# First up-projection of a fused encoder layer: convolution and gate in tiles of 1024 columns, two-column copies on ScalarE

## The chip, the cores and the metric

The kernel runs on one core of one Trainium2 chip. The metric is device time in microseconds (us) of one execution, from the first to the last instruction of the core. The time before is 2424.99 us, the median of 3 runs (2424.58 to 2426.9). Engines are called by their names in the profile: PE is the matmul array (TensorE), PEld its weight load, DVE is VectorE, ACT is ScalarE, POOL is GpSimd, SP issues most DMAs.

## What is computed

The reference is one layer over 2048 positions of width 1024: a projection, two groups of heads side by side (A: spatial gating; B: attention with forgetting over 8 heads of width 64), an out-projection with a residual, and a feed-forward part whose up-projection is followed by a causal convolution over three positions and a gate. Cut to what matters here:

```python
s = jnp.einsum('bhtd,bshd->bhts', qi, k) * scale + ci[..., :, None] - c[:, :, None, :]
p = jax.nn.softmax(jnp.where(kpos[None, :] <= qpos[:, None], s, -jnp.inf), axis=-1)
out_b = jnp.einsum('bhts,bshd->bthd', p, v)
x = x + jnp.concatenate([out_a, out_b], axis=-1) @ w_out

def conv_ffn(h, w_up, w_conv, b_conv, w_down):       # D_FF = 2816
    a = h @ w_up                                     # (positions, 2 * D_FF)
    a = causal_depthwise_conv3(a, w_conv) + b_conv   # position t uses t, t-1, t-2
    g, val = jnp.split(a, 2, axis=-1)
    return (jax.nn.silu(g) * val) @ w_down
x = x + conv_ffn(rms_norm(x, norm_ffn_g), w_up, w_conv, b_conv, w_down)
```

## The kernel before, in words

**Arithmetic.** All data are 32-bit floats. A product is made of three matmuls on a high and a low part of each operand (high by high, high by low, low by high): `mm3` (L206 to L214) issues 24 matmuls of 128x512, all on L212, and calls `tick()` after each.

**Stages, by the trace of before.** Projections of both halves of the positions (0 to 584 us); `c_half`, the out-projection of the first 1024 positions with its norm and its transposes (584 to 726); `d_half`, the first up-projection, for the same 1024 positions (726 to 1419); `c_late`, the out-projection of the last 1024 positions (1419 to 1575); then the rest of the up-projection and the down-projection (to 2424).

**The attention as fill.** Attention of the B heads has no stage of its own. It is a generator, and `tick()` advances it by one step (`step()`) after every so many matmuls: four numbers in `RATES`, one each for the two halves of the projections, for `c_half` and for `d_half`. For each block of 512 queries and each head there are two parts:

- `b_max` (L759 to L797), the score sweep. One matmul (L774) for 128 queries against 512 keys, and one VectorE instruction that takes the row's minimum (L777, or L779 with the mask of the diagonal block). 16 of these for the last query block.
- `b_mix` (L799 to L866), over chunks of 128 keys, 16 for the last query block. Per chunk two matmuls for the scores (L821, L822), the exponential on ScalarE (L827), a split of it into two parts (ScalarE L832, VectorE L833), a running sum on VectorE (L835), and two matmuls with the values (L809, L810). At the end of a head the sums go through a small matmul (L851) and a reciprocal (L852); after the second head of a pair four transposes (L186, of the tile `rw` from ScalarE L857) and the store to `mixh` and `mixl` in DRAM follow.

`need(tb)` (L137) drives the generator until query block tb is through; it stands in `c_half`, in the last pair of `d_half` and in `c_late`. After the one in `c_late` the last query block is read back (`load_mix(3)`), and a matmul of `c_late` on tile `thi` needs that. Of the 384 matmuls of `c_late`, 228 don't need the attention of that block and stand in front of this point.

A scheduler makes each engine's final order from all of this at build time; steps of the attention carry a priority 100 places ahead. The order is then fixed: every engine takes its instructions one after the other.

**The first up-projection.** There are 22 pairs of channel groups (f for the gate, 22 + f for the value), and two blocks of 512 positions. `d_up` (L920 to L949) handles one pair and one block. For each of the two channel groups: `mm3` into a bank of PSUM; ScalarE copies it to a tile `a` of 514 columns (L931) and makes `t`, the same values times the third tap plus the bias (L932); VectorE copies the two columns of the block before from `halo` to the front of `a` (L933) and the last two columns of `a` to `halo` (L934), and adds the two other taps (L935, L936). Then the gate: tanh on ScalarE (L943), and two VectorE instructions (L944, L947), the second into the tile `va`, which a DMA issued on POOL stores after block 1 (L949). `d_half` (L951 to L976) calls `d_up` for f = 0 and 1 over block 0 and then over block 1, the same for f = 20 and 21, and for the 18 others block 0 and block 1 at once. After the first pair it closes the pools of `c_half` and opens a pool that gives the attention more buffers. `d_sums` prepares weights on POOL for a later stage.

The late up-projection, after 1575 us, already does its convolution and gate in tiles of 1024 columns; its lines L1225, L1282, L1283 and L1287 to L1289 are used below as a measure.

Of the kernel before, what the change touches and what calls it, by code (L numbers as in the profile page):

```python
# [8 lines left out]
F32 = mybir.dt.float32  # L9
# [23 lines left out]
RATES = [3.5, 4.0, 4.4, 3.6]  # L33
# [48 lines left out]
class Block:  # L82
    def __init__(self, ctx, tc, ins, out):
        self.ctx, self.tc, self.nc, self.a, self.out = ctx, tc, tc.nc, ins, out
        self.uid = 0
        self.count = 0
        self.late = []
        self.va = {}
# [831 lines left out]
    def d_up(self, f, wg, wv, b):  # L920
        nc, dp, pp = self.nc, self.dp, self.dpp
        outs = []
        hT = self.hT[b]
        for ch, (wh, wl) in ((f, wg), (NF + f, wv)):
            ps = self.til(pp, [P, TB], F32, "mm")
            self.mm3(ps, [wh[:, k, :] for k in range(KC)], [wl[:, k, :] for k in range(KC)],
                     [hT[0][:, k, :] for k in range(KC)], [hT[1][:, k, :] for k in range(KC)])
            t = self.til(dp, [P, TB], F32, "t")
            a = self.til(dp, [P, TB + 2], F32, "a")
            cc = slice(ch, ch + 1)  # L930
            nc.scalar.activation(a[:, 2:TB + 2], ps, AF.Copy)  # L931
            nc.scalar.activation(t, ps, AF.Identity, scale=self.cw2[:, cc], bias=self.cb[:, cc])  # L932
            nc.vector.tensor_copy(a[:, 0:2], self.halo[:, ch, :])  # L933
            nc.vector.tensor_copy(self.halo[:, ch, :], a[:, TB:TB + 2])  # L934
            nc.vector.scalar_tensor_tensor(t, a[:, 1:TB + 1], self.cw1[:, cc], t, op0=ALU.mult, op1=ALU.add)  # L935
            nc.vector.scalar_tensor_tensor(t, a[:, 0:TB], self.cw0[:, cc], t, op0=ALU.mult, op1=ALU.add)  # L936
            outs.append(t)
            if ch == f:
                spare = a
        g, v = outs  # L940

        th = spare[:, 0:TB]
        nc.scalar.activation(th, g, AF.Tanh, scale=0.5)  # L943
        nc.vector.scalar_tensor_tensor(g, th, 1.0, g, op0=ALU.add, op1=ALU.mult)  # L944
        if b == 0:
            self.va[f] = self.til(dp, [P, D], F32, "va")
        nc.vector.tensor_tensor(self.va[f][:, b * TB:(b + 1) * TB], g, v, op=ALU.mult)  # L947
        if b:
            nc.gpsimd.dma_start(self.act_d[0][f], self.va.pop(f))  # L949

    def d_half(self):  # L951

        units = lambda f: [self.load_unit(self.a["w_up"][c], P) for c in (f, NF + f)]
        for f0 in range(0, NF, 2):
            if 0 < f0 < NF - 2:
                for f in (f0, f0 + 1):
                    w = units(f)
                    self.d_up(f, *w, 0)
                    if f > f0:
                        self.d_sums(f // 2)  # L960
                    self.d_up(f, *w, 1)
                continue
            ws = [units(f0), units(f0 + 1)]
            for k in range(2):
                self.d_up(f0 + k, *ws[k], 0)
# [4 lines left out]
            for k in range(2):  # L970
                self.d_up(f0 + k, *ws[k], 1)
            if not f0:
                self.flush()
                self.accs.close()
                self.bx = self.bxs.enter_context(self.tc.tile_pool(name="bxpool", bufs=1, side="right", reuse_waits="tile"))
                self.more = True  # L976
    def d_sums(self, i):
# [506 lines left out]
    def run(self):  # L1484
# [15 lines left out]
        dstack = ExitStack()  # L1500
# [58 lines left out]
```

## Time and profile before

| | |
|---|---|
| time, median of 3 runs | 2424.99 us |
| time of the profiled execution | 2425.66 us |
| its span | 2424.0 us |
| PE busy | 2375.0 us, 98% |
| DVE busy | 1900.7 us, 78% |
| ACT busy | 1150.2 us, 47% |
| POOL busy | 335.8 us, 14% |
| mean granted PE clock | 0.991 |

The span is the time from the first to the last instruction that the profiler recorded; 1.66 us of the execution lie around it. "Busy" counts the time in which an instruction runs on an engine. Matmuls overlap each other on PE: one of 128x512 is shown with 0.39 us, but the next may start 0.23 us after it, so a PE that is 98% busy need not be at its peak. The granted clock tells at which share of its full rate the array was let run. A stretch of the span is shown by a row of ten or so numbers, each engine's busy time with its count of instructions. "Idle before <- X" is the time for which an engine stood still ahead of an instruction, and X is what let it go on.

### The profile page before, as it was taken

The numbers are of one execution on the slowest core, as the hardware profiler recorded it, in microseconds if no ns is written. First come the engines' busy times: TensorE is split into PE (matmuls) and PEld (weight loads), VectorE is DVE, ScalarE is ACT, GpSimd is POOL, SyncE is SP. The second block draws the span as 40 slices with busy tenths as digits, with TensorE's granted clock in tenths as the row PEclk, the third lists the DMA queues.
The fourth block names the chain that finished last, engine by engine and source line by source line (L and its number), as shares of the span: only waits on it lengthen the run. The fifth ranks groups of instructions, "written<-read, shape, count | busy, mean of one in ns | idle before, by whom it ended". The sixth has DMA issues, their size and how long they took to land.

```text
span 2424.0 us, 32411 instructions
## 1 busy us (share of the span) xinstructions
PE 2375.0 (98%) x11224; PEld 1974.9 (81%) x11224; DVE 1900.7 (78%) x3324; ACT 1150.2 (47%) x1986; POOL 335.8 (14%) x315
## 2 busy tenths in 40 slices
PE   9999999999999999999999999899999999999998
PEld 7888888988778888888887887688888887888887
DVE  5357777866679988999999887598888877957875
ACT  4235655432424444454454435465555455454444
POOL 4114130101123222222222010100000000000001
PEclk9999999999999999999999999899999999999999
DMA  8663536658545444444444453312222228538633
GB/s 263 185 242 99 176 95 175 173 170 294 174 156 195 163 143 152 144 155 148 150 159 151 164 200 132 122 53 88 86 79 87 87 91 308 163 100 299 202 119 123
DMA packets 234517, 379.56 MB, mean 157 GB/s; under 512 B 49944, under 2 KB 109464, under 8 KB 232928
## 3 DMA queue, kind: packets, MB, share of 16 engines
q1 hardware_dynamic: 229312, 353.36, 45.3%
q0 software_dynamic: 5040, 24.12, 2.5%
q8 instruction: 89, 1.46, 0.3%
q14 instruction: 76, 0.62, 0.1%
HBM read 283.82 MB, written 93.72 MB: 156 GB/s over the span
## 4 chain that ended last, share of the span: by engine, by line
PE 83%; DVE 6%; DMA 5%; issue 3%; ACT 1%; POOL 1%; SPq 0%; POOLq 0%; DVEq 0%; ACTq 0%
PE mm L212 39%; PE D L1373 14%; PE A L1171 3%; PE A L1172 3%; PE A L1173 3%; PE o L810 2%; PE o L809 2%; PE s L774 2%; PE s L822 2%; PE s L821 2%; PE B L1172 2%; PE B L1173 2%; PE B L1171 2%; DVE sum L835 1%; PE C L1171 1%
## 5 line engine op out<-in xcount | busy, mean ns | idle before, releaser
L212 PE MATMUL mm<-tlo,whi 128*128 128x512 f32 x896 | 352.4, 394 | 0.0
L212 PE MATMUL mm<-thi,whi 128*128 128x512 f32 x896 | 351.9, 393 | 0.5 <-DVE vn L520 0.5
L212 PE MATMUL mm<-thi,wlo 128*128 128x512 f32 x896 | 352.0, 393 | 0.0
L212 PE MATMUL mm<-whi,thi 128*128 128x512 f32 (+2 forms) x768 | 279.3, 364 | 16.3 <-DMA thi<-mixh 9.0
L212 PE MATMUL mm<-wlo,thi 128*128 128x512 f32 (+2 forms) x768 | 277.3, 362 | 2.0 <-DVE wlo L165 2.0
L212 PE MATMUL mm<-whi,tlo 128*128 128x512 f32 (+2 forms) x768 | 275.8, 360 | 0.4 <-DMA tlo<-mixl 0.4
L151 POOL TENSOR_SCALAR whi<-raw 128x1024 fp32r<-128x1024 f32 (+3 forms) x114 | 144.3, 1267 | 915.0 <-PE mm L212 743.0
L212 PEld LDWEIGHTS mm<-thi,whi 128*128 128x128 f32 x896 | 168.6, 188 | 34.5 <-issue 0.7
L212 PEld LDWEIGHTS mm<-tlo,whi 128*128 128x128 f32 x896 | 168.6, 188 | 33.6
L212 PEld LDWEIGHTS mm<-thi,wlo 128*128 128x128 f32 x896 | 168.6, 188 | 33.1
L212 PEld LDWEIGHTS mm<-whi,thi 128*128 128x128 f32 x768 | 146.9, 191 | 37.6 <-DMA thi<-mixh 10.0
L835 DVE TENSOR_TENSOR sum<-sum,e 128x512 f32<-128x512 f32 (+3 forms) x249 | 161.7, 650 | 13.6 <-ACT e L827 10.6
L212 PEld LDWEIGHTS mm<-wlo,thi 128*128 128x128 f32 x768 | 147.2, 192 | 22.5 <-DVE wlo L165 2.9
L212 PEld LDWEIGHTS mm<-whi,tlo 128*128 128x128 f32 x768 | 146.7, 191 | 21.8 <-DMA tlo<-mixl 1.3
L165 DVE TENSOR_TENSOR wlo<-raw,whi 128x1024 fp32r<-128x1024 f32 (+2 forms) x106 | 131.5, 1241 | 33.7 <-POOL whi L151 33.4
L827 ACT ACTIVATE e<-s 128x512 f32<-128x512 f32 (+3 forms) x207 | 105.2, 518 | 108.5 <-DVE s L825 46.9
L1373 PE MATMUL D<-wl,xh 128*128 128x512 f32 x368 | 141.5, 389 | 0.0
L1373 PE MATMUL D<-wh,xh 128*128 128x512 f32 x368 | 140.8, 389 | 0.2 <-DVE xo L1474 0.2
L833 DVE TENSOR_TENSOR pl<-e,ph 128x512 fp32r<-128x512 f32 (+3 forms) x195 | 123.5, 637 | 21.1 <-PE o L810 13.9
L1373 PE MATMUL D<-wh,xl 128*128 128x512 f32 x368 | 137.7, 389 | 0.0
L832 ACT ACTIVATE ph<-e 128x512 fp32r<-128x512 f32 (+3 forms) x195 | 105.4, 549 | 46.1 <-PE o L809 39.1
L931 ACT ACTIVATE a<-mm 128x512 f32<-128x512 f32 x88 | 52.6, 598 | 122.3 <-PE mm L212 118.3
(1837 smaller groups left out, 5756.4 us busy)
## 6 DMA issues: line engine op xcount, KB each, us to landing
raw<-in_w_up_dram SPq DMA_DIRECT2D x72, 512.0 KB
m<-kx SPq DMA_DIRECT2D x160, 136.0 KB
x<-act SPq DMA_DIRECT2D x84, 256.0 KB
m<-kx SPq DMA_DIRECT2D x67, 256.0 KB
v<-vd SPq DMA_DIRECT2D x67, 256.0 KB
raw<-in_w_in_dram SPq DMA_DIRECT2D x28, 512.0 KB
raw<-in_w_out_dram SPq DMA_DIRECT2D x24, 512.0 KB
tw<-in_w_down_dram SPq DMA_DIRECT2D x11, 1024.0 KB
```

The costliest lines, as they stand in the source:

```text
L151: self.cast_ins = self.nc.gpsimd.tensor_scalar(out, in_, 1.0, 0.0, ALU.mult, ALU.add).ins
L165: nc.vector.tensor_tensor(lo, raw, f32(hi), op=ALU.subtract)
L212: self.last_mm = self.nc.tensor.matmul(ps, lhsT=a[k], rhs=b[k], start=i == 0, stop=i == 3 * n - 1).ins
L827: nc.scalar.activation(e[:, c], ps[:, c], AF.Exp, scale=-1.0)
L832: nc.scalar.activation(ph[:, c], e[:, c], AF.Copy)
L833: nc.vector.tensor_tensor(pl[:, c], e[:, c], f32(ph[:, c]), op=ALU.subtract)
L835: nc.vector.tensor_tensor(total[:, c], total[:, c], e[:, c], op=ALU.add)
L931: nc.scalar.activation(a[:, 2:TB + 2], ps, AF.Copy)
L1171: mm(ps, lhsT=xh[:, ks], rhs=yh[:, k, :], start=fresh and k == 0, stop=False, **kw)
L1172: mm(ps, lhsT=xh[:, ks], rhs=yl[:, k, :], start=False, stop=False, **kw)
L1173: mm(ps, lhsT=xl[:, ks], rhs=yh[:, k, :], start=False, stop=k == 3, **kw)
L1373: nc.tensor.matmul(bank[t], lhsT=x[i][:, ts], rhs=w[k], start=fresh and j == 0 and i + k == 0, stop=last and i == 1, **kw)
```

## The change

1. **Wide tiles.** For f = 2 to 19 (`d_wide`) the two blocks of a channel pair now share one tile `a` of 1026 columns and one tile `t` of 1024. ScalarE still empties each bank of PSUM as before, 512 columns at a time, but the taps, the tanh and the two gate instructions are done once, over 1024 columns, after block 1. The result is written over the value's `t`, and the DMA stores it from there; the tile `va` is gone.
2. **The first and the last pair** (f = 0, 1, 20, 21; `d_blocks`) keep their order and their width of 512. Their four calls share two tiles `a` and the halves of one tile `t`.
3. **Two-column copies** (to and from `halo`) move from VectorE to ScalarE.
4. **Buffers.** Instead of 2 `a`, 4 `t` of 512 and 2 `va`, 2 `a` and 3 `t` of 1024, and one more of each in a pool that is opened after the first pair.
5. **Rates** of the attention fill: 3.8 instead of 4.0 matmuls for one step in the second half of the projections, 4.0 instead of 4.4 in `c_half`, 3.5 instead of 3.6 in `d_half`.

The program has 3042 VectorE instructions instead of 3326 and 2010 ScalarE instructions instead of 1924. PE, POOL and SP keep their numbers.

```diff
-RATES = [3.5, 4.0, 4.4, 3.6]
+RATES = [3.5, 3.8, 4.0, 3.5]
...
-    "ar": 4, "a": 2, "t": 4, ... "tw": 1, "s0": 1, "va": 2, "e+": 1, ...
+    "ar": 4, "a": 2, "t": 3, "a+": 1, "t+": 1, ... "tw": 1, "s0": 1, "e+": 1, ...
...
-    def d_up(self, f, wg, wv, b):
...
+    def d_channel(self, ch, w, b, a, t):
+        nc = self.nc
+        hT, (wh, wl) = self.hT[b], w
+        ps = self.til(self.dpp, [P, TB], F32, "mm")
+        self.mm3(ps, [wh[:, k, :] for k in range(KC)], [wl[:, k, :] for k in range(KC)],
+                 [hT[0][:, k, :] for k in range(KC)], [hT[1][:, k, :] for k in range(KC)])
+        nc.scalar.activation(a, ps, AF.Copy)
+        nc.scalar.activation(t, ps, AF.Identity, scale=self.cw2[:, ch:ch + 1], bias=self.cb[:, ch:ch + 1])
+
+    def d_conv(self, ch, a, t, n):
+        nc = self.nc
+        cc = slice(ch, ch + 1)
+        nc.scalar.activation(a[:, 0:2], self.halo[:, ch, :], AF.Copy)
+        nc.scalar.activation(self.halo[:, ch, :], a[:, n:n + 2], AF.Copy)
+        nc.vector.scalar_tensor_tensor(t, a[:, 1:n + 1], self.cw1[:, cc], t, op0=ALU.mult, op1=ALU.add)
+        nc.vector.scalar_tensor_tensor(t, a[:, 0:n], self.cw0[:, cc], t, op0=ALU.mult, op1=ALU.add)
+
+    def d_gate(self, th, g, v, out):
+        nc = self.nc
         nc.scalar.activation(th, g, AF.Tanh, scale=0.5)
         nc.vector.scalar_tensor_tensor(g, th, 1.0, g, op0=ALU.add, op1=ALU.mult)
+        nc.vector.tensor_tensor(out, g, v, op=ALU.mult)
+
+    def d_blocks(self, f, ws, b, a, t, out):
+        halves = t[:, 0:TB], t[:, TB:HALF]
+        for j in range(2):
+            self.d_channel(f + j * NF, ws[j], b, a[j][:, 2:TB + 2], halves[j])
+            self.d_conv(f + j * NF, a[j], halves[j], TB)
+        self.d_gate(a[0][:, 0:TB], *halves, out[:, b * TB:(b + 1) * TB])
+
+    def d_wide(self, f, ws, b):
         if b == 0:
+            self.wide = []
+        for j in range(2):
+            if b == 0:
+                self.wide.append((self.d_tile("a"), self.d_tile("t")))
+            a, t = self.wide[j]
+            self.d_channel(f + j * NF, ws[j], b, a[:, 2 + b * TB:2 + (b + 1) * TB], t[:, b * TB:(b + 1) * TB])
+            if b:
+                self.d_conv(f + j * NF, a, t, HALF)
         if b:
+            (a, g), (_, v) = self.wide
+            self.d_gate(a[:, 0:HALF], g, v, v)
+            self.nc.gpsimd.dma_start(self.act_d[0][f], v)
```

The scheduler lays out the whole program anew, so that the attention stands elsewhere among the matmuls. Two places show it. A number behind a tile's name only tells one tile of that name from another, and the lines of the changed kernel are one less than before for code that is the same (L211 for L212, L773 for L774, L776 for L777, L821 and L820 for L822 and L821).

**The tail of the attention, on PE.** The first place is the last matmul of `c_late` that can run before the last query block is read back, and what follows it. Before, the rows behind it are chunks of `b_mix`:

```order
L212 MATMUL mm_15131<-whi_14875,thi_14851 128x512
L212 MATMUL mm_15131<-wlo_14876,thi_14851 128x512
L212 MATMUL mm_15131<-whi_14875,tlo_14853 128x512
L810 MATMUL o_12972<-pl+_3050_13172,v+_3034_13116 128x512
L809 MATMUL o_12972<-ph+_3055_13193,v_13183 128x512
L821 MATMUL dn_13334<-t_49_401,m_48_400 128x512
L822 MATMUL dn_13334<-t_3076_13291,m_3079_13296 128x512
L821 MATMUL dn_13348<-t_49_401,m_48_400 128x512
```

In the changed kernel a score sweep comes first:

```order
L211 MATMUL mm_14821<-whi_14565,thi_14541 128x512
L211 MATMUL mm_14821<-wlo_14566,thi_14541 128x512
L211 MATMUL mm_14821<-whi_14565,tlo_14543 128x512
L773 MATMUL dn_12558<-m_47_399,t_49_401 128x512
L185 MATMUL s_12493<-ident,rw_12487 128x128 x4
L773 MATMUL s_12511<-m_48_400,t_49_401 128x512
L773 MATMUL s_12537<-m_48_400,t_49_401 128x512
L773 MATMUL dn_12564<-m_47_399,t_49_401 128x512
```

From there to the transposes of the last `rw`, which are followed by the matmuls that need the last query block, the order before has 16 matmuls of L821, 16 of L822, 20 of L809, 21 of L810 and 8 of L851: the end of one head and one whole head. In the changed kernel there are 14 of the score sweep (L773), the transposes of an earlier pair, 32 each of the four lines of `b_mix`, and 8 of L850: nearly a whole score sweep and two whole heads. The last 156 matmuls of the out-projection stand behind it in both.

**The convolution, on VectorE.** The second place lies in the middle of `d_half`. Before, the instructions of one channel and block stand between attention instructions of the same width, and the two-column copies stand among them:

```order
L933 COPY a_9792<-halo 128x2
L794 TENSOR_TENSOR t_50_402<-s_7945,rowsel 8x512
L934 COPY halo<-a_9719 128x2
L935 SCALAR_TENSOR_TENSOR t_9718<-a_9719,cols,t_9718 128x512
L835 TENSOR_TENSOR sum_7891<-sum_7891,e_7951 128x512
L936 SCALAR_TENSOR_TENSOR t_9718<-a_9719,cols,t_9718 128x512
```

In the changed kernel (L941 and L942 are the taps, L948 is the gate, L776 the minimum of the score sweep):

```order
L941 SCALAR_TENSOR_TENSOR t_10728<-a_10727,cols,t_10728 128x1024
L776 TENSOR_REDUCE part_8490<-s_8505 128x1
L942 SCALAR_TENSOR_TENSOR t_10728<-a_10727,cols,t_10728 128x1024
L776 TENSOR_REDUCE part_8490<-s_8511 128x1
L776 TENSOR_REDUCE part_8490<-s_8519 128x1
L847 TENSOR_TENSOR op_8476<-o_8243,op_8476 64x512
L948 SCALAR_TENSOR_TENSOR t_10728<-a_10727,t_10728 128x1024
```

The copies are gone from VectorE, and an attention instruction now waits for one tap of 1024 columns instead of 512; each tap stands once for two blocks.

More of the change, by code (lines that the diff above doesn't have):

```diff
@@ L87, in __init__ @@
         self.late = []
-        self.va = {}
         self.fill = None
@@ new lines, in d_tile @@
+    def d_tile(self, tag):
+        n = self.nd[tag] = self.nd.get(tag, -1) + 1
+        late = self.more and n % (BUFS[tag] + BUFS[tag + "+"]) >= BUFS[tag]
+        return self.til(self.d2 if late else self.dp, [P, HALF + 2 if tag == "a" else HALF], F32, tag + "+" if late else tag)
+    def d_channel(self, ch, w, b, a, t):
[6 more added lines that the diff above has]
+        nc.scalar.activation(t, ps, AF.Identity, scale=self.cw2[:, ch:ch + 1], bias=self.cb[:, ch:ch + 1])
@@ L957, in d_half @@
                     w = units(f)
-                    self.d_up(f, *w, 0)
+                    self.d_wide(f, w, 0)
                     if f > f0:
                         self.d_sums(f // 2)
-                    self.d_up(f, *w, 1)
+                    self.d_wide(f, w, 1)
                 continue
             ws = [units(f0), units(f0 + 1)]
+            out = [self.d_tile("t") for _ in range(2)]
+            t, a = self.d_tile("t"), [self.d_tile("a") for _ in range(2)]
             for k in range(2):
-                self.d_up(f0 + k, *ws[k], 0)
+                self.d_blocks(f0 + k, ws[k], 0, a, t, out[k])
             self.d_sums(f0 // 2)
```

32 lines of the change are left out of this document (6 added, 26 removed), and 2 rows, old and new, of the table BUFS.

## Prediction

> **What bounds the kernel now.** I read the page first, for the span and the busy time of the engines.
>
> ```profile
> span 2424.0 us, 32411 instructions
> PE 2375.0 (98%) x11224; PEld 1974.9 (81%) x11224; DVE 1900.7 (78%) x3324; ACT 1150.2 (47%) x1986; POOL 335.8 (14%) x315
> ```
>
> PE is busy nearly throughout, VectorE for 78%. As that is a mean over stages, the table by windows comes next: the out-projection of the first half, the up-projection that is changed, and the end of the attention. A row has start, end and length, the busy time of PE, PEld, DVE, ACT and POOL with counts, the granted PE clock, and the DMA's share and GB/s.
>
> ```profile
> 584.00:726.00 142.00, 132.93 (x599) 106.86 (x599) 93.62 (x172) 45.08 (x86) 30.20 (x31) 0.94 0.59 190
> 726.00:1419.00 693.00, 688.71 (x3166) 569.21 (x3165) 637.42 (x1194) 329.38 (x600) 153.58 (x125) 1.00 0.49 161
> 1492.00:1535.00 43.00, 31.74 (x126) 21.56 (x125) 26.02 (x50) 27.98 (x48) 3.49 (x8) 0.80 0.33 117
> 1496.20:1516.20 20.00, 17.58 (x63) 10.37 (x61) 18.93 (x37) 16.23 (x31) 0.00 (x0) 0.91 0.16 51
> 633.40:640.20 6.80, 5.28 (x13) 4.15 (x14) 0.00 (x0) 1.72 (x3) 0.10 (x1) 0.50 0.61 200
> ```
>
> In the up-projection VectorE is very full (637.42 of 693 us, 92%), yet PE stands idle for only 693 - 688.71 = 4.29 us, at the full clock. At the end of the attention it is the other way round: in 20 us from 1496.2, VectorE works for 18.93 us and PE has gaps, at a clock of 0.91. So the third view is the table of waits of PE, first for the up-projection alone (total, times, longest):
>
> ```profile
> PE o L810 <- DVE pl L833: 2.4, 3, 1.2
> PE s L851 <- DVE sum L835: 1.2, 1, 1.2
> PE s L821 <- DVE t L794: 0.6, 1, 0.6
> ```
>
> That is 4.2 us: nearly all the idle time of that stage is a wait for VectorE, and there is hardly any. For the whole span:
>
> ```profile
> PE mm L212 <- DMA thi<-mixh: 9.0, 2, 7.2
> PE o L810 <- DVE pl L833: 4.0, 6, 1.2
> PE s L822 <- DMA v<-vd: 3.2, 1, 3.2
> PE s L774 <- DVE part L777: 2.9, 4, 1.0
> ```
>
> The 7.2 us are the read of the last query block behind the attention's end. The timeline of PE shows that end (start, length, engine, line, tiles, and idle time with its releaser):
>
> ```profile
> 1491.74 0.39 PE L810 MATMUL o<-pl+_3050_13172,v+_3034_13116 128*128 128x512 f32 x1
> ...
> 1492.19 0.39 PE L821 MATMUL dn<-t,m 128*128 128x512 f32 x1
> 1492.42 0.39 PE L822 MATMUL dn<-t,m 128*128 128x512 f32 x1
> ...
> 1517.79 1.12 PE L186 MATMUL dn<-ident,rw 128*128 128x128 f32 x4 [1.22 <-ACT rw L857]
> ```
>
> Back to back, full matmuls start 0.23 us apart. From 1491.74, where the last matmul that needs no attention has just been issued, to 1517.79 there are 26.05 us of attention alone, which I call the tail. Its pace on VectorE:
>
> ```profile
> 1496.25 1.29 DVE L833 TENSOR_TENSOR pl<-e,ph 128x512 fp32r<-128x512 f32 x2 [0.37 <-ACT ph L832]
> ...
> 1500.24 0.68 DVE L835 TENSOR_TENSOR sum<-sum,e 128x512 f32<-128x512 f32 x1
> 1500.84 0.69 DVE L833 TENSOR_TENSOR pl+_3104_13377<-e,ph+_3103_13376 128x512 fp32r<-128x512 f32 x1
> ...
> 1515.85 0.29 DVE L835 TENSOR_TENSOR sum<-sum,e+_3162_13591 128x128 f32<-128x128 f32 x1
> 1516.17 0.69 DVE L848 TENSOR_TENSOR op<-o,op 64x512 f32<-64x512 f32 x1
> ```
>
> VectorE instructions start 0.60 us apart (1500.24 to 1500.84), and the 16 chunks of one head take it from 1496.25 to 1515.85 + 0.29 = 1516.14: 19.9 us, in which PE has only 64 matmuls of 0.23 us or less, at most 14.7 us. So the up-projection is bound by PE, the tail by VectorE.
>
> **VectorE and ScalarE, part by part.** The groups by line (count | busy in us, mean ns | idle before). First what is there now, then the same work at 1024 columns from the late up-projection, then ScalarE's tanh at both widths and its nearest tiny copy.
>
> ```profile
> L933 DVE COPY a<-halo 128x2 f32<-128x2 f32 x88 | 29.3, 333 | 0.4
> L934 DVE COPY halo<-a 128x2 f32<-128x2 f32 x88 | 20.0, 227 | 18.1 <-ACT a L931 17.8
> L935 DVE SCALAR_TENSOR_TENSOR t<-a,cols,t 128x512 f32<-128x512 f32 x88 | 69.8, 793 | 5.3 <-ACT t L932 5.3
> L936 DVE SCALAR_TENSOR_TENSOR t<-a,cols,t 128x512 f32<-128x512 f32 x88 | 70.8, 804 | 0.9
> L944 DVE SCALAR_TENSOR_TENSOR t<-a,t 128x512 f32<-128x512 f32 x44 | 32.8, 745 | 7.1 <-ACT a L943 6.9
> L947 DVE TENSOR_TENSOR va<-t,t 128x512 f32<-128x512 f32 x44 | 34.7, 789 | 0.3
> L1282 DVE SCALAR_TENSOR_TENSOR ts<-cv,cols,ts 128x1024 f32<-128x1024 f32 x44 | 55.8, 1283 | 29.8 <-ACT ts L1281 29.8
> L1283 DVE SCALAR_TENSOR_TENSOR ts<-cv,cols,ts 128x1024 f32<-128x1024 f32 x44 | 56.0, 1282 | 0.8
> L1288 DVE SCALAR_TENSOR_TENSOR ts<-cv,ts 128x1024 f32<-128x1024 f32 x22 | 26.8, 1219 | 0.0
> L1289 DVE TENSOR_TENSOR ts<-ts 128x1024 f32<-128x1024 f32 x22 | 26.8, 1218 | 0.0
> L943 ACT ACTIVATE a<-t 128x512 f32<-128x512 f32 x44 | 27.8, 632 | 87.0 <-DVE t L936 82.4 <-DVE rr L852 2.4 <-DVE mx L784 2.3
> L1287 ACT ACTIVATE cv<-ts 128x1024 f32<-128x1024 f32 x22 | 23.3, 1059 | 18.0 <-DVE ts L1283 18.0
> L1225 ACT ACTIVATE cv<-halo 128x4 f32<-128x4 f32 x22 | 4.5, 203 | 9.0 <-DVE ts L1288 8.2 <-DVE t2l L1013 0.6
> ```
>
> VectorE loses the six groups: 29.3 + 20.0 + 69.8 + 70.8 + 32.8 + 34.7 = 257.4 us. It gets 18 wide pairs of 2 x (1.283 + 1.282) + 1.219 + 1.218 = 7.57 us, 136.2 together, and 8 narrow ones (4 pairs, 2 blocks) of 2 x (0.793 + 0.804) + 0.745 + 0.789 = 4.73 us, 37.8 together. Net: 174.0 - 257.4 = -83 us, so about 554 of 693 us. ScalarE gets 2 x (18 x 2 + 4 x 2 x 2) = 104 copies of 0.203 us, 21.1 us, and its tanh falls from 27.8 to 18 x 1.059 + 8 x 0.632 = 24.1; net +17, on 329.38 of 693 us.
>
> On the path these 83 us are worth next to nothing: PE issues the same matmuls, and all that VectorE can give back there is the 4.2 us of waits. I take half, **-2 us**. Bounds: -4.3, the whole idle time of the stage, and +4, as many new waits. New ones are possible. On VectorE an attention instruction can now be queued behind a tap of 1.28 us (was 0.79), and PE's next matmul of that chunk waits for it. On ScalarE the copies follow their eviction on the same engine and wait for nothing else, but a tanh that waits for VectorE's taps (82.4 us of idle time now, in front of L943) waits for taps of 1.28 us, with the exponentials L827 queued behind it, for which L835, L833 and then PE's L809 wait. The cover is the 139 us in which VectorE will be free.
>
> The narrow pairs share tiles over their calls, so an eviction waits until the gate of the call before has read its tile. A call's two groups of 24 matmuls last 24 x 0.23 = 5.5 us each, its gate 0.632 + 0.745 + 0.789 = 2.2 us, so it is covered. If VectorE is late by 0.5 us in each of the 8 calls, that is again the +4. The store from `v`, with `t` free only when it is done, has a pair's 4 x 5.5 = 22 us of matmuls as its cover.
>
> **The out-projection of the first half** keeps its order nearly unchanged: **0 us**, with bounds of -6.6 (the 3.2 us wait for `v` goes, and with it half of the 6.8 us at clock 0.50, first fence) and +4 (as much again of the 3.2, rounded up).
>
> **The tail.** Here the order weighs. The changed kernel has a score sweep and two heads where before had about one. Two minima of a sweep, on the timeline of VectorE:
>
> ```profile
> 666.61 1.28 DVE L777 TENSOR_REDUCE part<-s 128x1 f32<-128x512 f32 x2
> ```
>
> The masked one by its group:
>
> ```profile
> L779 DVE CUSTOM_DVE_ANT_0 s<-s,mask 128x384 f32<-128x384 f32 (+3 forms) x113 | 53.3, 495 | 15.5 <-PE s L774 15.2
> ```
>
> Two minima take 1.28 us, one every 0.60. For 14 of a sweep: 10 x 0.60 + 4 x 0.5 = 8.0 us, and three instructions that close the pair of heads before (row 1516.17) at 0.60 = 1.8; together 10 us. Then two heads of 19.9. Ahead of all this I put 1 us, and at the end 1517.79 - 1516.14 = 1.65 us, as before. New tail: 1 + 10 + 39.8 + 1.65 = 52.4 us, against 26.05: +26.4.
>
> What was moved into the tail is gone from among the matmuls in front of it, where PE is the bound. Of the score sweep that is 14 matmuls, 10 full and 4 masked ones worth 2.5: 12.5 x 0.23 = 2.9 us. A head has 12 full chunks and 4 on the diagonal worth 2.5, so 14.5 x 4 = 58 full matmuls. Two heads make 116; before, one head and some 6 of the head ahead of it stood there, 64. The 52 more are 12.0 us. Together -14.9, and the difference is +11.5. A longer stretch with gaps also meets more of the slower clock seen there; from 0.91 in 20 us I estimate +1.5 for 26 us more. The tail: **+13 us**. Its lower bound is +1.5, if the sweep's 10 us run wholly beside other VectorE gaps. Its upper bound is 11.5 + 4 (clock) + 3.5 (VectorE starting 1496.25 - 1491.74 = 4.5 us late, as now, and not 1) = +19.
>
> **The rates** act only through the order and are in it; the read of 7.2 us stays, since its place is the same.
>
> Sum: -2 + 0 + 13 = +11. Profiled execution 2425.7 + 11 = 2436.7 us; the median of the runs lies 0.67 us below that execution, so **2436.0 us**.
>
> **Rivals.** *A, VectorE was the bound after all.* Its relief takes away PE's waits for it: 4.0 + 2.9 + 1.2 + 0.6 = 8.7 us, so 2416. For it speaks the 92%; against it, that matmuls start 0.23 us apart and only 4.29 us of 693 are idle. It decides if the tail costs less than 8.7 - 4.85 (0.2%, below) = 3.9 us. The Trainium skill, "Perfetto Trace Analysis", section "Identifying the Most-Contended Engine", ranks VectorE by its occupancy, but TensorE by the busy share of its weight loads. By that rule VectorE (92%) stands above TensorE (569.21 / 693 = 82%) and should be relieved first; the trace's idle time contradicts it for this stage. Chance 0.10.
>
> *B, the tail is hidden, or the change isn't seen.* The work was only moved, and gaps of the old tail take it in: for one head VectorE needs 19.9 us and PE 14.7, so a moved head costs at most 5 us more than it freed, and the 4 us of waits in the up-projection and the sweep's overlap pay for that: 2425 + 5 - 4 = about 2426, 4.8 us either way. Against it: in the tail VectorE has no gap (18.93 of 20). Chance 0.15.
>
> *C, the array at half rate in the tail (slower than forecast).* With gaps in the matmuls the clock falls, as in 1492 to 1535 (0.80). A full chunk's four matmuls take 4 x 0.227 = 0.91 us at full rate and 1.82 at half, above VectorE's 1.20; a head's 14.5 x 1.82 = 26.4 us in place of 19.9, +6.5 for each of two heads: 2436 + 13 - 1.5 = about 2447. It decides as soon as PE can't keep 0.60 us per VectorE instruction. The Trainium skill, "TensorE: Matmul & The Clock Gate", section "Part 1: The HAM clock gate (the "warmup" mystery)", says that an idle window of some 3.4 us halves the array's clock and a busy one brings it back. By that rule the tail, whose gaps are under 1 us, should keep its clock; the 0.91 shows that it lost some. Chance 0.13.
>
> **Chances and range.** Forecast 0.62, A 0.10, B 0.15, C 0.13. The measurement can tell about 0.2%, 4.85 us, so "same" reaches from 2420 to 2430. It gets most of B (0.12) and the low end of the forecast (0.04); faster gets A and the rest of B worth telling (0.11); slower keeps 0.73. With the tail's two ends the forecast alone reaches from 2425 - 2 + 1.5 = 2424.5 to 2425 - 2 + 19 = 2442, with +4 of new waits 2446. The range reaches over B's lower half and to C's time: 2421 to 2447; below it lies A, above it the worse half of C.
>
> **What would show it.** In the changed profile: VectorE falls by about 83 us and ScalarE gains 17 in the up-projection; PE's idle time there stays at 4 us or less; the last `rw` transposes come about 52 us after the last free matmul, with VectorE some 90% busy between; the wait of 7 us for `thi` remains. I am wrong if that stretch lasts under 40 us, if new waits in the up-projection exceed 4 us, or if the out-projection of the first half moves by more than 4.

## The result, and the profile after

The changed kernel takes 2451.76 us (median of 4 runs, 2448.04 to 2453.75) against 2425.56 us for the kernel before on the same chip (2424.58 to 2426.9): a ratio of 1.0106, with a 95% interval of 1.0094 to 1.0118. It is slower by 26 us. The forecast was 2436, with a range of 2421 to 2447: the right side, and too small. Its profiled execution took 2450.7 us.

The page, span and busy time by engine:

```profile
span 2449.0 us, 32182 instructions
PE 2385.1 (97%) x11224; PEld 1981.1 (81%) x11224; DVE 1860.2 (76%) x3040; ACT 1161.0 (47%) x2072; POOL 339.4 (14%) x315
```

PE has the same 11224 matmuls. VectorE has 40.5 us less to do (1900.7 to 1860.2), ScalarE 10.8 more. So the 25 us of span are idle time and lost clock of PE, and the question is where.

To find them, count the matmuls of the three projections (line L212, L211 after the change; `mm3`) as mile posts: they are the same 4992 in both kernels. Between two posts I take the time and subtract the PE work of all matmuls started there, 0.227 us for each 512 columns, with 0.06 us as the least of one. What remains is the excess: idle time, slower clock, everything that isn't work.

| stretch | excess before | after |
|---|---|---|
| projections (to matmul 2112) | 47.4 | 45.6 |
| out-projection, first half (2112 to 2496) | 24.3 | 24.8 |
| first up-projection, start (2496 to 2700) | 4.9 | 8.5 |
| first up-projection, rest (2700 to 4608) | 19.2 | 19.6 |
| second out-projection, free matmuls (4608 to 4836) | 2.2 | 2.1 |
| **tail: last free matmul to the first that needs the last query block (4836 to 4837)** | **18.6** | **42.4** |
| the rest, to the last matmul | 12.3 | 11.0 |
| sum | 128.9 | 154.0 |

Of the 25.1 us, 23.8 lie in the tail. The next number, 3.6, is at the start of the up-projection. In the long stretch, which holds nearly all of the change, the excess hardly moves: 19.2 and 19.6.

The same by windows: first the up-projection and the tail before, then after (start, end, length; PE, PEld, DVE, ACT, POOL busy; PE clock; DMA share; GB/s).

```profile
723.70:1409.30 685.60, 681.31 (x3133) 563.22 (x3132) 630.09 (x1183) 321.84 (x586) 153.94 (x125) 1.00 0.48 158
1491.50:1526.10 34.60, 23.78 (x96) 15.54 (x94) 23.17 (x45) 25.47 (x46) 3.49 (x8) 0.83 0.23 76
```

```profile
720.70:1394.00 673.30, 666.31 (x3052) 548.56 (x3051) 559.28 (x844) 317.07 (x641) 158.89 (x124) 1.00 0.47 154
1479.20:1552.50 73.30, 49.45 (x169) 34.33 (x167) 53.01 (x104) 42.16 (x80) 3.48 (x8) 0.75 0.27 87
1482.00:1503.00 21.00, 13.35 (x33) 8.63 (x33) 12.68 (x28) 5.07 (x10) 0.00 (x0) 0.59 0.17 55
```

In the up-projection VectorE goes from 630.09 to 559.28 us and PE's idle time is 4.29 us before, 7.0 after. The tail grows from 34.6 to 73.3 us, and its clock falls to 0.75; from 1482 to 1503 us it is 0.59, and VectorE works for only 12.68 of 21 us there. So the tail isn't at VectorE's pace near its start. In the whole tail PE is idle for 34.6 - 23.78 = 10.8 us before and 73.3 - 49.45 = 23.9 after. Of the 23.8 us of excess 13.0 are therefore idle time, and the other 10.8 lie in PE's busy time, which gets longer where the clock is lower. The waits of PE in the tail after the change say what it waits for:

```profile
PE mm L211 <- DMA thi<-mixh: 7.0, 1, 7.0
PE dn L820 <- DMA m<-kx: 4.1, 2, 2.6
PE dn L773 <- DMA m<-kx: 3.0, 2, 1.8
PE o L809 <- DVE pl L832: 2.0, 4, 0.7
PE dn L820 <- ACT ph L831: 2.0, 1, 2.0
PE s L820 <- DMA m<-kx: 1.9, 1, 1.9
```

The read of the last block (7.0) was there before. New are 4.1 + 3.0 + 1.9 = 9.0 us of waits for `m`, the tile of 512 keys that both the score sweep and the chunks read. The timeline of PE in the tail:

```profile
1479.23 0.40 PE L211 MATMUL mm<-whi,tlo 128*128 128x512 f32 x1
1479.46 0.40 PE L773 MATMUL dn<-m,t 96*128 96x512 f32 x1
...
1484.19 0.50 PE L773 MATMUL dn<-m,t 96*128 96x512 f32 x1 [1.20 <-DMA m<-kx]
...
1486.93 0.47 PE L773 MATMUL dn<-m,t 96*128 96x128 f32 x1 [1.78 <-DMA m<-kx]
...
1491.09 1.22 PE L820 MATMUL dn<-t,m 128*128 128x512 f32 x2 [2.61 <-DMA m<-kx]
...
1497.20 1.22 PE L820 MATMUL dn<-t,m 128*128 128x512 f32 x2 [1.46 <-DMA m<-kx]
...
1544.38 1.12 PE L185 MATMUL dn<-ident,rw 128*128 128x128 f32 x4 [1.04 <-ACT rw L856]
```

Each of these waits for `m` is at the change from one key block to the next. And the queue that loads the blocks, SP's, waits itself (window 1480 to 1506):

```profile
SPq L100 <- PE s L773: 8.2, 2, 5.3
SPq L100 <- PE s L820: 7.2, 1, 7.2
SPq L100 <- PE dn L773: 2.3, 1, 2.3
SPq L100 <- DVE pl+_2875_12500 L199: 1.5, 1, 1.5
SPq L100 <- DMA m<-kx: 1.3, 1, 1.3
SPq L100 <- ACT ph+_2874_12499 L198: 1.3, 1, 1.3
```

There are two tiles `m`. A load can't be issued before PE has done with the block that lay in the tile (L773, L820), and the stores of the pair of heads before (L198, L199) stand in the same queue ahead of it. While the attention is spread among free matmuls, nobody waits for that. Alone in the tail, it does: a sweep needs a new block every 4 score matmuls, 4 x 0.60 = 2.4 us at VectorE's pace.

### The profile page after: what moved, and what is told of

It is laid out like the page before. It is cut to its first block, busy times and chain, and to the rows that moved or that the text cites. A ratio compares the mean times of both kernels' runs of the same rounds, so it can differ in the third digit from the quotient of the medians.

```text
span 2449.0 us, 32182 instructions
## 1 busy us (share of the span) xinstructions
PE 2385.1 (97%) x11224; PEld 1981.1 (81%) x11224; DVE 1860.2 (76%) x3040; ACT 1161.0 (47%) x2072; POOL 339.4 (14%) x315
## 4 chain that ended last, share of the span: by engine, by line
PE 83%; DMA 6%; DVE 5%; issue 2%; ACT 2%; POOL 2%; SPq 0%; POOLq 0%; DVEq 0%; ACTq 0%
PE mm L211 37%; PE D L1404 16%; PE A L1202 3%; PE A L1204 3%; PE A L1203 3%; PE o L809 2%; PE o L808 2%; PE s L773 2%; PE B L1203 2%; PE B L1204 2%; PE B L1202 2%; PE s L821 2%; PE s L820 2%; DMA tw<-in_w_down_dram 1%; DVE sum L834 1%
## 5 line engine op out<-in xcount | busy, mean ns | idle before, releaser
L211 PE MATMUL mm<-thi,whi 128*128 128x512 f32 x896 | 353.5, 395 | 0.5 <-DVE vn L519 0.5
L211 PE MATMUL mm<-tlo,whi 128*128 128x512 f32 x896 | 351.8, 393 | 0.0
L211 PE MATMUL mm<-thi,wlo 128*128 128x512 f32 x896 | 351.8, 393 | 0.0
L211 PE MATMUL mm<-whi,thi 128*128 128x512 f32 (+2 forms) x768 | 278.7, 364 | 15.3 <-DMA thi<-mixh 9.2
L211 PE MATMUL mm<-whi,tlo 128*128 128x512 f32 (+2 forms) x768 | 276.4, 361 | 3.3 <-DMA tlo<-mixl 3.3
L211 PE MATMUL mm<-wlo,thi 128*128 128x512 f32 (+2 forms) x768 | 277.0, 361 | 2.0 <-DVE wlo L164 2.0
L150 POOL TENSOR_SCALAR whi<-raw 128x1024 fp32r<-128x1024 f32 (+3 forms) x114 | 137.5, 1208 | 827.2 <-PE mm L211 580.3
L211 PEld LDWEIGHTS mm<-thi,whi 128*128 128x128 f32 x896 | 168.6, 188 | 34.6 <-issue 0.7
L211 PEld LDWEIGHTS mm<-thi,wlo 128*128 128x128 f32 x896 | 168.6, 188 | 33.4
L211 PEld LDWEIGHTS mm<-tlo,whi 128*128 128x128 f32 x896 | 168.7, 188 | 33.3
L164 DVE TENSOR_TENSOR wlo<-raw,whi 128x1024 fp32r<-128x1024 f32 (+2 forms) x106 | 136.4, 1289 | 53.4 <-POOL whi L150 50.6
L211 PEld LDWEIGHTS mm<-whi,thi 128*128 128x128 f32 x768 | 146.9, 191 | 36.0 <-DMA thi<-mixh 9.9
L211 PEld LDWEIGHTS mm<-whi,tlo 128*128 128x128 f32 x768 | 146.6, 191 | 24.4 <-DMA tlo<-mixl 4.2
L211 PEld LDWEIGHTS mm<-wlo,thi 128*128 128x128 f32 x768 | 147.0, 191 | 22.8 <-DVE wlo L164 2.9
L776 DVE TENSOR_REDUCE part<-s 128x1 f32<-128x512 f32 x146 | 95.7, 681 | 33.0 <-PE s L773 32.5
```

Of the source, the lines that this page charges most:

```text
L150: self.cast_ins = self.nc.gpsimd.tensor_scalar(out, in_, 1.0, 0.0, ALU.mult, ALU.add).ins
L164: nc.vector.tensor_tensor(lo, raw, f32(hi), op=ALU.subtract)
L211: self.last_mm = self.nc.tensor.matmul(ps, lhsT=a[k], rhs=b[k], start=i == 0, stop=i == 3 * n - 1).ins
L776: nc.vector.tensor_reduce(dst, ps, axis=AX.X, op=ALU.min)
```

## The experiments

Two theories for the 25 us. **Tail**: the new order leaves more attention for the tail, and the time follows what is left there. **Wide tiles**: instructions of 1024 columns, their bursts after block 1, the shared tiles or the ScalarE copies cost time where they stand. How many attention matmuls of L773, L820, L821, L808 and L809 (and their counterparts in the other kernels) stand in the tail can be counted in each kernel's order: 73 before, 142 after. The small matmuls that close a head (L851 before, L850 after) aren't counted; the traces have 16 of them in either tail, two heads' worth, where the account of the order above has 8.

| kernel | in the tail | tail, us | excess in it | excess, rest of up-projection | median, us | ratio to before (95%) |
|---|---|---|---|---|---|---|
| before | 73 | 34.6 | 18.6 | 19.2 | 2425.6 | |
| after | 142 | 73.3 | 42.4 | 19.6 | 2451.8 | 1.0106 (1.0094 to 1.0118) |
| 1 copies only | 29 | 18.0 | 11.9 | 23.1 | 2422.0 | 0.9982 (0.9973 to 0.9992) |
| 2 rates only | 85 | 40.1 | 21.9 | 25.2 | 2435.5 | 1.0034 (1.0022 to 1.0045) |
| 3 wide, halved, old rates | 30 | 18.6 | 12.2 | 16.7 | 2418.4 | 0.9968 (0.9958 to 0.9978) |
| 4 after, no key loads | 142 | 63.4 | 32.5 | 19.9 | 2445.7 | 1.0080 (1.0064 to 1.0095) |
| 5 before, short attention | 0 | 0.2 | 0.0 | 21.3 | 2347.0 | 0.9672 (0.9652 to 0.9693) |
| 6 wide, old rates, short attention | 0 | 0.2 | 0.0 | 17.7 | 2348.9 | 0.9681 (0.9659 to 0.9703) |
| 7 wide, old rates | 145 | 71.7 | 40.2 | 17.4 | 2450.2 | 1.0096 (1.0077 to 1.0114) |
| 8 per block, old rates | 0 | 8.2 | 7.8 | 24.9 | 2420.6 | 0.9967 (0.9956 to 0.9979) |
| 9 as 3, rate 3.3 | 129 | 57.6 | 29.6 | 14.9 | 2431.5 | 1.0021 (1.0011 to 1.0031) |
| 10 taps halved, gate wide | 73 | 34.9 | 18.9 | 17.8 | 2424.2 | 0.9992 (0.9982 to 1.0002) |
| 11 after, VectorE copies | 138 | 65.0 | 35.2 | 18.6 | 2443.3 | 1.0069 (1.0052 to 1.0086) |

The kernel before took 2426.4 to 2426.5 us beside the experiments. Excess is worked out from each profiled execution as above.

**1. The copies alone.**

```diff
-            nc.vector.tensor_copy(a[:, 0:2], self.halo[:, ch, :])
-            nc.vector.tensor_copy(self.halo[:, ch, :], a[:, TB:TB + 2])
+            nc.scalar.activation(a[:, 0:2], self.halo[:, ch, :], AF.Copy)
+            nc.scalar.activation(self.halo[:, ch, :], a[:, TB:TB + 2], AF.Copy)
```

> The kernel before with one part of the change: the two-column copies on ScalarE. In its order the attention runs ahead of where it was: 29 matmuls of the chunks are left behind the last free matmul, where the kernel before has 73 and the changed one 142. Tail theory (the time follows from how much attention is left for the tail): the measured tails, 26.05 us for 73 and 64.9 us for 142, make 0.56 us per matmul, of which 0.23 us are saved in front of the tail; 44 fewer x 0.33 us = 15 us less, 2411 us, at least 10 us less. Wide-tile theory (the 25 us come from the taps of 1024 columns and their bursts): nothing here is wide, so no change but the copies' own, 2425 us within 3.

4.4 us faster: the sign that the tail theory gave, and a third of the size (10 at least were expected). 2422.0 us is also just inside the 2425 within 3 of the other theory, so this run doesn't decide between them. In the tail 6.7 us of excess went; the slope of 0.33 us per matmul was too steep, since the end of the tail (transposes, and 7.0 us for the read of the last block) stays whatever is in front. In the up-projection 3.9 us came back.

**2. The rates alone.**

```diff
-RATES = [3.5, 4.0, 4.4, 3.6]
+RATES = [3.5, 3.8, 4.0, 3.5]
```

> The kernel before with one part of the change: the four new rates. 85 matmuls of the chunks are left for the tail, 12 more than before. Tail theory: 12 x 0.33 = +4 us, about 2429 us. Wide-tile theory: no change, 2425 us. Too close to tell the two apart alone; what it tells is the share of the rates in the 25 us: at most 4 by either.

9 us slower, more than either theory gave. The tail holds 3.3 of it; the excess at the start of the up-projection went from 4.9 to 10.2 and in its rest from 19.2 to 25.2. In this kernel the rates cost more in front of the tail than in it.

**3. Wide tiles and bursts, instructions of 512, old rates.** The four wide taps and the two wide gate instructions of a pair are cut in two:

```diff
+        if n == HALF:
+            for q in (slice(0, TB), slice(TB, HALF)):
+                nc.vector.scalar_tensor_tensor(t[:, q], a[:, 1 + q.start:1 + q.stop], self.cw1[:, cc], t[:, q], op0=ALU.mult, op1=ALU.add)
+                nc.vector.scalar_tensor_tensor(t[:, q], a[:, q], self.cw0[:, cc], t[:, q], op0=ALU.mult, op1=ALU.add)
+            return
...
+        for q in ((slice(0, TB), slice(TB, HALF)) if g.shape[-1] == HALF else (slice(0, TB),)):
+            nc.vector.scalar_tensor_tensor(g[:, q], th[:, q], 1.0, g[:, q], op0=ALU.add, op1=ALU.mult)
+            nc.vector.tensor_tensor(out[:, q], g[:, q], v[:, q], op=ALU.mult)
```

> The changed kernel with the old rates, and with each wide VectorE instruction of the convolution and gate cut in two of 512 columns, still all after block 1, in the same tiles and with the copies on ScalarE. VectorE does the same elements as in the kernel before, in the bursts of the changed kernel. 30 matmuls are left for the tail. Tail theory: 43 fewer than before x 0.33 = 14 us less, 2411 us. Wide-tile theory in the form that the bursts after block 1, the shared tiles or the ScalarE copies cost the time: slower than 2440 us; in the form that only the length of 1.28 us costs it: 2425 us.

8 us faster than before, about halfway between the 2411 of the tail theory and the 2425 of instruction length alone. Over 2440 us was expected if the bursts after block 1, the shared tiles or the ScalarE copies cost the time; all three are in this kernel, so they don't. Against run 7, which differs only in the length of the instructions, it is 32 us.

**4. Without the key loads.** In `b_keys`, for heads 6 and 7 of the last query block:

```diff
-        self.dma(f32(m1[0:68, :]), self.kx[hf][h, 64:132, sl])
+        if not skip:
+            self.dma(f32(m1[0:68, :]), self.kx[hf][h, 64:132, sl])
...
-            nc.scalar.activation(e[:, c], ps[:, c], AF.Exp, scale=-1.0)
+            nc.scalar.activation(e[:, c], ps[:, c], AF.Exp, scale=0.0 if tb == 3 and h >= 6 else -1.0)
```

> The changed kernel without the loads of the key tile m (the 68 rows from kx, the one of two tiles) for the last two heads of the last query block, which then use what lies in it; their exponential is taken with scale 0, so that it stays finite. Same order of PE in the tail, 142 matmuls. Key-load theory (part of the tail's 64.9 us is waits for m, 9 us in the profile, and the half clock that follows them): the tail gets 9 to 17 us shorter, total 2435 to 2443 us. VectorE theory (the tail has the length that VectorE needs, and PE would wait for VectorE instead): 2448 to 2452 us, as the changed kernel.

The tail is 9.9 us shorter (73.3 to 63.4), within the 9 to 17 expected. The total, 2445.7, is only 6.1 us shorter and lies between the two forecasts for it (2435 to 2443, and 2448 to 2452): by the excess, part of the gain was lost again elsewhere, 1.4 us of it at the start of the up-projection (9.9 against 8.5). The waits of PE and the window of its tail:

```profile
PE mm L211 <- DMA thi<-mixh: 7.6, 1, 7.6
PE o L810 <- DVE pl L833: 2.4, 6, 0.7
PE s L821 <- ACT e L827: 1.2, 3, 0.5
PE o L809 <- ACT ph L832: 1.1, 1, 1.1
PE dn L185 <- ACT rw L857: 1.0, 1, 1.0
```

```profile
1481.80:1545.20 63.40, 46.01 (x170) 28.96 (x168) 52.33 (x104) 43.29 (x81) 3.48 (x8) 0.88 0.26 82
```

No wait for `m` is left, the clock is 0.88 instead of 0.75, and VectorE is busy for 52.33 of 63.4 us (53.01 of 73.3 before). The excess that remains, 32.5, is 13.9 above that of the kernel before. The order inside the tail isn't quite the same (scores and chunks alternate more), so the 9.9 us are the loads and what the scheduler made of their absence.

**5 and 6. No tail at all.** Four heads of the last query block see only their last 512 keys, in the kernel before (5) and in the changed kernel with the old rates (6). The edit is the same in both:

```diff
-        for sb in range(tb + 1):
+        s0 = 12 if tb == 3 and h >= 4 else 0
+        for sb in range(s0 // 4, tb + 1):
...
-        for sc in range(ns):
+        for sc in range(s0, ns):
```

> The kernel before, with part of the attention left out: the last four heads of the last query block see only the last 512 keys (36 of its 128 chunk steps and the sweeps over them are gone for them, 12 chunks and 12 sweep steps per head). No tail is left: all attention stands in front of the last free matmuls. PE work removed: 4 heads x (12 x 4 + 12) x 0.227 = 54.5 us; the excess of the tail, 19.0 us of idle time and slower clock there, falls to about 2. 2426 - 54 - 17 = 2355 us by both theories (2350 to 2362); this is the base for the run beside it.

> The changed kernel with the old rates and the same part of the attention left out, so that it has wide tiles, wide VectorE instructions and ScalarE copies, but no tail either. Tail theory: the wide tiles cost nothing once the tail is gone, so the same time as the run beside it within 3 us, about 2355 us. Wide-tile theory: the 25 us are paid in the up-projection, so about 20 us more than the run beside it, 2375 us.

2347.0 and 2348.9 us: 1.9 us apart, with ranges that overlap (2345.8 to 2348.3 and 2345.2 to 2353.2), where the full kernels of the same rates, before and run 7, are 23.7 us apart. The level is 8 us below what I had worked out. The up-projection of the two:

```profile
721.30:1398.40 677.10, 673.03 (x3131) 558.09 (x3130) 615.28 (x1179) 319.89 (x590) 152.82 (x125) 1.00 0.47 157
```

```profile
723.70:1391.40 667.70, 663.37 (x3054) 548.85 (x3053) 561.17 (x847) 320.06 (x651) 158.36 (x125) 1.00 0.47 157
```

54 us less on VectorE in run 6, and 4.07 us of PE's idle time in one, 4.33 in the other. About 20 us of difference were expected if the wide tiles cost the time where they stand. Without a tail they cost nothing that these ranges, 3 and 8 us wide, can tell, and bring nothing either.

**7. The changed kernel with the old rates.**

```diff
-RATES = [3.5, 3.8, 4.0, 3.5]
+RATES = [3.5, 4.0, 4.4, 3.6]
```

> The changed kernel with the rates of before, all else as changed. 145 matmuls of chunks are left for the tail, as many as in the changed kernel (142). Tail theory: the tail costs its 24 us more than before, but the +4 us of the out-projection of the first half, which the run with the rates alone shows too (excess 19.6 to 27.1 us behind it, 14.7 to 11.7 ahead of it), go: about 2447 us. If the rates were the cause: 2430 us or less.

2450.2 us: 1.5 less than with the new rates, where 4 were expected, and with overlapping intervals. So the rates that cost 9 us alone cost next to nothing on top of the wide tiles, and they aren't the cause of the 25 us.

**8. The changed kernel's tiles, convolution per block.** `d_conv` and `d_gate` are called for each block of 512 on its part of the wide tiles, with the old rates; halo copies only before block 0 and after block 1.

```diff
-            if b:
-                self.d_conv(f + j * NF, a, t, HALF)
+            self.d_conv(f + j * NF, a[:, o:o + TB + 2], t[:, q], TB, b == 0, b == 1)
...
+        (a, g), (_, v) = self.wide
+        self.d_gate(a[:, q], g[:, q], v[:, q], v[:, q])
```

> The changed kernel's tiles of 1024 columns and its copies on ScalarE, but convolution and gate once per block of 512 as before, with the old rates. Between the two blocks of a pair no copy is needed, as they lie side by side in one tile. The order leaves no tail: no run of 18 attention matmuls, 4 matmuls of the out-projection come after the last of them. Tail theory: the excess of 19.0 us in the tail falls to some 10 (the read of the last block, 7 us, can't be hidden by 4 matmuls), about 2416 us. Wide-tile theory, in the form that tiles and copies cost the time: over 2435 us.

2420.6 us, 6 less than before, where 10 were expected: the tail's excess fell to 7.8, of which 7.0 is the read of the last block; 5.7 came back in the up-projection.

**9. One rate, same instructions as 3.**

```diff
-RATES = [3.5, 4.0, 4.4, 3.6]
+RATES = [3.5, 4.0, 4.4, 3.3]
```

> The run with halves of 512 columns and the old rates again, with one number changed: 3.3 instead of 3.6 matmuls for one step of the attention in the up-projection. All instructions are the same. In the order 129 matmuls of chunks are left for the tail instead of 30. Tail theory, with the excess measured so far in the tail (12.5 us for 30, 19.0 for 73, 22.3 for 85, 40.6 for 145): 36 us for 129, 24 us more than with 30, about 2442 us. Wide-tile theory: nothing is wide, 2418 us within 4.

13 us more than run 3, with the same instructions and no wide one, and 17.4 us more excess in the tail (12.2 to 29.6). So more attention in the tail costs time by itself. The 24 us expected leaned on the 40.6 us of run 7, whose tail begins with a score sweep; here only 1 sweep matmul is in it (14 after the change), and the waits of PE for `m` are 2.1 us over the whole span:

```profile
PE mm L211 <- DMA thi<-mixh: 8.8, 2, 7.0
PE mm L211 <- DVE vn L519: 6.3, 3, 5.2
PE o L809 <- DVE pl L832: 5.2, 7, 2.0
PE s L773 <- DVE part L776: 2.8, 4, 0.9
PE dn L820 <- DMA m<-kx: 2.1, 1, 2.1
```

**10. Only the taps halved**, the gate wide, old rates: the first half of the diff of run 3.

> The changed kernel with the old rates, with only the four taps of a wide pair cut into halves of 512; the gate's two instructions stay at 1024. 73 matmuls are left for the tail, as many as in the kernel before. Tail theory: the same excess there, 19 us, and the same time as before, 2426 us within 4, although VectorE has some 40 us less to do than before and ScalarE some 17 more. If VectorE's load mattered: 2418 us or less.

2424.2 us, no difference from before (interval 0.9982 to 1.0002), with the same 73 matmuls and 34.9 us of tail, although VectorE is busy for 31.6 us less (1900.7 to 1869.1) and ScalarE for 7.1 more (1150.2 to 1157.3). By VectorE's load 2418 us or less were expected.

**11. The wide kernel with the copies on VectorE.**

```diff
-        nc.scalar.activation(a[:, 0:2], self.halo[:, ch, :], AF.Copy)
-        nc.scalar.activation(self.halo[:, ch, :], a[:, n:n + 2], AF.Copy)
+        nc.vector.tensor_copy(a[:, 0:2], self.halo[:, ch, :])
+        nc.vector.tensor_copy(self.halo[:, ch, :], a[:, n:n + 2])
```

> The changed kernel with the two-column copies back on VectorE. 138 matmuls are left for the tail. Tail theory: the excess of the tail is that of the changed kernel less 1 or 2 us, 2449 to 2452 us, so that the copies have no part in the 25 us. If the copies on ScalarE cost time in the up-projection: 5 us or more less, 2446 us or below.

2443.3 us, 8 less than the changed kernel: a miss of the expectation. But the up-projection isn't where it is saved (18.6 against 19.6); the tail's excess is 35.2 instead of 42.4. Four sweep matmuls fewer stand in it (10 instead of 14), so it seems that the copies act through the order here too, in the other direction than in run 1.

## Why the forecast was right in its side and wrong in its size

**"On the path these 83 us are worth next to nothing: -2 us."** Right in that VectorE's relief brings nothing: the excess of the up-projection's long stretch is 19.2 before and 19.6 after, and runs 5 and 6 show it without the tail. The sign for it, that PE's idle time there stays at 4 us or less, didn't hold. It rose to 7.0, still within the bound of 4 us of new waits: PE's waits for VectorE went from 4.2 to 5.7 us, and 1.1 for the exponential came up.

The 83 us themselves were 40.5 on the page, for three reasons. By their durations the taps and gates take 184.3 us, 10.3 more than the 174.0 worked out, and the other instructions 10.0 more than before. The rest, 22.6, was never there to gain: VectorE instructions overlap their neighbours by a little, so that the durations of all of them make 2111.0 us before and 2047.9 after, and the busy times only 1900.7 and 1860.2. Adding up groups counted this overlap twice. The first tap of 34 of the 52 is shown here:

```profile
L941 DVE SCALAR_TENSOR_TENSOR t<-a,cols,t 128x1024 f32<-128x1024 f32 (+1 forms) x34 | 40.0, 1178 | 0.6 <-ACT t L933 0.5
L164 DVE TENSOR_TENSOR wlo<-raw,whi 128x1024 fp32r<-128x1024 f32 (+2 forms) x106 | 136.4, 1289 | 53.4 <-POOL whi L150 50.6 <-PE mm L211 2.5
```

It would be 18 x 1.283 + 16 x 0.793 = 35.8 us by the forecast's rows, and the weights' low parts (L164) take 4.9 us more than before (131.5, 106 of them). As VectorE had 673.30 - 559.28 = 114 us free there, little of it mattered. Why these instructions are dearer wasn't tried.

**"The out-projection of the first half: 0 us."** Right: 24.3 and 24.8. Just behind it 3.6 us were lost (4.9 to 8.5). Run 2 shows 5.3 there with the new rates alone, run 7 only 1.8 with the old rates and wide tiles, so about half of it is the rates' work. I had said that "the rates act only through the order and are in it"; that place I hadn't looked at.

**"The tail: +13 us, bounds +1.5 and +19."** This is the step that failed, in its size: +23.8. The tail was to take 52.4 us from the last free matmul to the last `rw` transposes, and took 1544.38 - 1479.46 = 64.9; VectorE was to be some 90% busy in it, and was busy for 50.03 of these 64.9 us, 77%. I priced the score sweep at VectorE's pace ("10 x 0.60 + 4 x 0.5 = 8.0 us"), the two heads behind it likewise, and put the loads of their keys at nothing. But PE and VectorE both waited: the key blocks, through two tiles, didn't come at that pace. From the first to the last matmul of the sweep 1492.96 - 1479.46 = 13.5 us passed. PE waited 9.0 us for `m`, 3.0 of them in the sweep and 6.0 in the chunks behind it (L820), and the clock was 0.75 over the tail against 0.83.

The rest of the term was about right. Run 4, without those loads, has +13.9 of excess in the tail over the kernel before, where the forecast had +13. The table gives the same without that edit. Tails with at most one sweep matmul lie near a line: 12.2 us of excess for 30 attention matmuls (run 3), 18.6 and 18.9 for 73, 21.9 for 85, 29.6 for 129 (run 9), which is (29.6 - 12.2) / 99 = 0.18 us for each. Continued to 142 it estimates 31.9 us. Run 4 has 32.5, and the changed kernel, with its 14 sweep matmuls and its loads, 42.4. Runs 7 and 11, with 14 and 10 sweep matmuls, lie above the line too, by 8 and 4 us. So of the 23.8 us some 13 are the attention that was moved, and some 10 are the loads and the lower clock that comes with their waits. The trace of before has no wait for `m` in its tail, and no sweep matmul; the tail of run 9, with one, has 2.1 us of such waits. A bound for the loads could have been put at one wait of a few us for each new block of keys; here the longest was 2.6 us. Whether a third tile `m`, or the stores on another queue, would remove the waits wasn't tried.

**The rivals.** *A* (VectorE as the bound) falls: 40.5 us less on VectorE, and the waits of PE for it in the up-projection didn't fall; in runs 5 and 6 a difference of 54 us on VectorE made none in the time. The rule of the Trainium skill ("Perfetto Trace Analysis", section "Identifying the Most-Contended Engine") would have relieved VectorE first by the busy share of the weight loads, which is all that the forecast took from it; beside that share the section names, for TensorE, the share of the peak arithmetic rate that is used. In this stage PE's 4 us of idle time were the better guide. *B* (the tail is hidden, about 2426) falls: the tail is where the time was lost. *C* (half rate in the tail) came in part: its sum of 2447 was near, and the clock did fall, to 0.50 from 1485 to 1502 us. But it fell among the waits for `m`; in run 4, without them, the clock of the tail was 0.88, higher than before the change.

**Why the tail got longer.** By the runs it is the length of the VectorE instructions, of the taps and of the gate: with both at 1024 columns 145 matmuls are left for the tail (run 7), with the gate alone wide 73 (run 10), with both in halves 30 (run 3), all with the old rates. What the scheduler does with it is not shown: a likely reading is that in its plan the attention's short VectorE steps stand behind longer ones, so that the matmuls of the up-projection overtake them. Nor is the count a smooth function: one rate of 3.3 instead of 3.6 takes the halved kernel from 30 to 129 (run 9). It is the tail that decides the time; what decides the tail stays open beyond these counts.

**A better kernel.** Runs 3 and 8 are the fastest, by 0.3% against before (0.9968, interval 0.9958 to 0.9978; 0.9967, interval 0.9956 to 0.9979): the copies on ScalarE and the shared tiles with instructions of 512.

## What to carry to other kernels

Where a scheduler lays out filler work by readiness, an edit on an engine that has time to spare can still cost time, by where it leaves the filler: count in the new order how much of it stands behind the last work that doesn't need it, before anything else. Price such a stretch not by its busiest engine alone but by every load in it that was hidden until now, with its round trip through the buffers it reuses. Parts of a change that act through one order don't add up: the rates cost 9 us alone and at most a few on top of the wide tiles, the copies gained 4 alone and lost 8 there.

## What the runs showed of the hardware

The array's clock fell to 0.59 over 1482 to 1503 us although no gap of PE in it was longer than 2.61 us, after 1.00 throughout the up-projection. The Trainium skill, "TensorE: Matmul & The Clock Gate", section "Part 1: The HAM clock gate (the "warmup" mystery)", gives an idle window of some 3.4 us as the condition, and further down in the same section tells of a kernel whose short idle times between groups of matmuls made the clock go back and forth. In these traces several shorter gaps in a row were enough. After the change the clock was 1.00 until 1485.1 us and 0.50 from there to 1502.1; in the 3.4 us ahead of the fall PE was busy for 1.92, and its longest gap was 1.20 us. Before the change it fell at 1510.6 us, in the tail as well; in the 3.4 us ahead PE was busy for 1.97, and its longest gap was only 0.67 us. No busy share that decides can be read from this: in run 7 PE was busy for 1.67 of the 3.4 us from 1516.6, and the clock stayed at 1.00 in them and behind them. So for a stretch with many gaps of 0.5 to 1 us the slower clock should be priced as a possibility, even where none of them is long.
